# Latent attention: one maximum tile issued after the whole fourth score, and a new assignment of four PSUM areas

## The chip, the core and the metric

The kernel runs on one core of a Trainium2 chip. The metric is the device time of one execution in microseconds (us), the median of several runs. The core has five instruction queues that matter here: the tensor engine (PE, with its weight loads shown apart as PEld), the vector engine (DVE), the scalar engine (ACT), GpSimd (POOL) and the queue that issues DMAs (SP). Each works through its own list in order; semaphores hold an instruction back until what it needs has happened on another engine. PE writes its products to PSUM, which the kernel holds as one tile `PB` of eight banks of 512 fp32 numbers per partition; DVE and ACT read them there.

## The reference, cut to what matters

A stream of 1024 latent tokens and 256 context tokens passes two layers: windowed attention, then multi-head latent attention. The change lies in the second. Its core, for 16 heads and all 1280 keys, is

```
s = (einsum("bqhd,bkhd->bhqk", qn, kn) + einsum("bqhd,bkd->bhqk", qr, kr)).astype(F32) * scale
p = softmax(s, axis=-1)
o = einsum("bhqk,bkhd->bqhd", p, v)
yx = (o * silu(gx)) @ w_out          # then residual and a last rms_norm
```

Only the latent tokens are queries, since no layer follows.

## The kernel before, in words

Layer 2's attention is cut into 32 units (`UnitB`): 16 heads, each with two halves of 512 queries. A unit's work is written as small steps, and the loop over units interleaves steps of neighbouring units by hand. PE, ACT and DVE run in exactly the order in which the code issues instructions (`manual_schedule`), so the text of the loop is the order of the queues. Waits between engines are derived by the framework from the tiles and regions that two instructions share.

The steps of a unit `u`, with `nu` the next one, `nnu` the one after that, and `pu` the one before:

- `top(b)`, for b = 0 to 3: an upper estimate of the scores of 128 queries, one plain product pass. Four matmuls (L1261) fill two banks, `psm`, with the scores against 1024 keys; the matmuls go in pairs, one on the upper and one on the lower 64 rows of the array, side by side. DVE takes the maximum over both banks (`reduce_max`, L1263). For b = 1 and b = 2, four more matmuls of 256 columns (L1269) then fill `rest`, the scores of two query blocks against the other 256 keys, and DVE reduces these too (L1270). For b = 3 a DVE minimum (L1272) joins the two. I call L1261 the maxima's products, and `rest` the paired parts.
- `shift()`: transposes the maxima into `pm_bank` (L1276) and builds the rows that are subtracted inside the score product (L1277, L1282).
- `score(i)`, for i = 0 to 4: 256 keys against 512 queries, five passes of a split-precision product, each a pair of matmuls: ten matmuls (L1298) into a slot of two banks. `score(i, a, b)` issues passes a to b-1 only. After the fifth, ACT takes the exponential of the slot into an SBUF tile (L1304), and POOL adds it to a running sum (L1308, L1312).
- `PV()`: the value product of the unit before, ten fp32 matmuls (L1320, recorded as 20) into `pv_bank`; ACT and DVE read it (L1335, L1339 in `fin` and `fin1`). `fin2` and `fin3` transpose the sums and apply them (L1349, L1364, L1365, L1367).

There are two slots, banks 4 and 5 and banks 6 and 7, handed out in turn by `slot()`: six times per unit (five scores and one scratch slot `x`). So score 0 of a unit takes the slot that score 3 of the unit before used, and score 1 that of score 4. The first matmul into a slot waits until the exponential that last read it is done.

The order on PE in one unit of the loop (L1544 to L1583) is: score 0 passes 0 and 1; `nu.top(2)`; the rest of score 0; score 1; `nu.top(3)`; in two of four units a product that builds the next heads' keys; the value product; the transposes; `nnu.top(0)`; score 2; score 3 passes 0 to 3; `nnu.top(1)`; score 3 pass 4; score 4. Every eighth unit builds values (`make_V`) ahead of `nnu.top(0)`.

The PSUM areas before:

| area | what | banks |
|---|---|---|
| `pv_bank` | value product | 0, all columns |
| `psm` (used part) | maxima's products | 1 and 2 |
| `pm_bank` | transposed maxima | 3, columns 0 to 127 |
| `rest` | paired parts | 0 and 3, columns 256 to 511 |
| `slots` | scores, scratch | 4 and 5, 6 and 7 |

Of the kernel before, what the change touches and what calls it, by code (L numbers as in the profile page):

```python
# [34 lines left out]
class Ring:  # L35
# [6 lines left out]
    def next(self):  # L42
        b = self.bufs[self.i % len(self.bufs)]
        self.i += 1
        return b
# [15 lines left out]
def kernel(ctx: ExitStack, tc: tile.TileContext, t, out, dbg=None):  # L61
# [5 lines left out]
    PB = ppool.tile([128, 8, 512], F32, name="PB")  # L67
# [56 lines left out]
    def mm3(o, a, b, first, last):  # L124
        (ah, al), (bh, bl) = a, b
        nc.tensor.matmul(o, ah, bh, start=first, stop=False)  # L126
        nc.tensor.matmul(o, al, bh, start=False, stop=False)  # L127
        nc.tensor.matmul(o, ah, bl, start=False, stop=last)  # L128
# [1021 lines left out]
    otr = Ring(F, [0, 4], 1024)  # L1150
    rbr = Ring(F, [8, 9], 256)
    mxr = Ring(F, [44, 44.5], 128)
    psm = PB[:, 1:4, :]
    pm_bank = PB[:, 3, 0:128]
    slots = [PB[:, 4:6, :], PB[:, 6:8, :]]
    pv_bank = PB[:, 0, :]
    rest = PB[:, 0:4:3, 256:512]

    def slot():
        slots.reverse()  # L1160
        return slots[1]

    def make_kr():
        for n, c0 in enumerate((0, 4, 8)):
            pt = slot()[:, 0]
            cn = min(4, NT - c0)
            for c in range(cn):
                nc.tensor.transpose(pt[0:32, c * 128 : c * 128 + 128], krF[:, c0 + c, :], ident)
            w = slice(512 * (n // 2), 512 * (n // 2) + 128 * cn)
            ps = [64 * t for t in ((0, 1) if n == 2 else (n,))]  # L1170
            src = pt[0:32, 0 : cn * 128]
            for p in ps:
                nc.scalar.copy(kr1[p : p + 32, w], src)
                nc.scalar.copy(kr2[n // 2][p : p + 32], src)
            for p in ps:
                nc.vector.tensor_sub(kr1[p + 32 : p + 64, w], src, kr1[p : p + 32, w].bitcast(F32))
            yield

    def ones_kr():
        for p in (32, 96):  # L1180
            for kr in kr2:
                n = kr.shape[-1]
                nc.gpsimd.tensor_copy(kr[p : p + 4], const[p : p + 4, 0:1].to_broadcast([4, n]))

    def make_V(quad, x, x0=psm[:, 0:2]):
        for t0, ps in ((0, x0), (4, PB[:, 0:1]), (2, x)):
            nt = min(2, NP - t0)
            for j in range(2 * nt):
                ti = 2 * t0 + j
                o = ps[:, j // 2, (j % 2) * 256 : (j % 2) * 256 + 256]  # L1190
                for k in range(2):
                    mm3(
                        o,
                        [ckvT[:, s, k, ti * 128 : ti * 128 + 128] for s in range(2)],
                        [ukV[:, s, k, quad * 256 : quad * 256 + 256] for s in range(2)],
                        k == 0, k == 1,
                    )
            nc.scalar.copy(
                Vq[:, 2 * t0 : 2 * t0 + 2 * nt].rearrange("p t h d -> p (t h d)"),
                ps[:, 0:nt].rearrange("p a b -> p (a b)"),  # L1200
            )
            yield
# [26 lines left out]
    class UnitB:  # L1229
# [24 lines left out]
        def top(self, b):  # L1254
            n, r1, _ = self.q
            bs = slice(b * 128, b * 128 + 128)
            pairs = ((n[:, 0, bs], self.kt[:, 0]), (r1[:, bs], kr1))
            rs = [slice(64 * t, 64 * t + 64) for t in range(2)]
            for i, (q, k) in enumerate(pairs):
                for t in range(2):  # L1260
                    nc.tensor.matmul(psm[:, t], q[rs[t]], k[rs[t], 0:512], start=i == 0, stop=i == 1)  # L1261
            mx, flat = self.mx, psm[:, 0:2].rearrange("p a b -> p (a b)")
            nc.vector.reduce_max(mx[:, 32 + b : 33 + b], flat, AX.X, negate=True)  # L1263
            if b in (1, 2):
                b0 = b - b % 2
                for i, (q, k) in enumerate(((n[:, 0], self.kt[:, 0]), (r1, kr1))):
                    for t in range(2):
                        c = slice((b0 + t) * 128, (b0 + t) * 128 + 128)
                        nc.tensor.matmul(rest[:, t], q[rs[t], c], k[rs[t], 512:768], start=i == 0, stop=i == 1)  # L1269
                nc.vector.reduce_max(mx[:, 104 + b0 : 106 + b0], rest, AX.X, negate=True)  # L1270
            if b == 3:
                nc.vector.tensor_tensor(mx[:, 32:36], mx[:, 32:36], mx[:, 104:108], ALU.min)  # L1272
# [209 lines left out]

    units = [UnitB(i) for i in range(NU)]
    vk = make_V(0, slots[0], slots[1])
    for m in mxr.bufs:
        nc.vector.memset(m, 0.0)
# [10 lines left out]
    with tc.manual_schedule(engines={E.PE, E.Activation, E.DVE}):  # L1497
        kr = make_kr()
        ones_kr()
        next(kr)  # L1500
        next(kr)
        g_tile(8, 3, 0, pv_bank)
        next(kr)
        g_tile(8, 3, 1)
        make_K(0, (0, 1), slot())
        g_tile(9, 3, 0, psm[:, 0])
        make_K(0, (2,), slot())
        g_tile(9, 3, 1)
        next(vk)
        u0.top(0)  # L1510
        next(vk)
        g_tile(8, 4, 0, slots[0][:, 0])
        u0.top(1)
        next(vk)
        u0.top(2)
        g_tile(8, 4, 1)
        units[2].prep()
        u0.top(3)
        g_tile(9, 4, 0, slots[0][:, 1])
        u0.shift()  # L1520
        u1.top(0)
        make_K(1, (0, 2), slots[1])
        u1.top(1)
        g_tile(9, 4, 1)
        nc.scalar.activation(warm, const[:, 1:2], AF.Exp)
        u1.top(2)
        for ui, u in enumerate(units):
            pu, ppu = [units[ui - n] if ui >= n else None for n in (1, 2)]
            nu, nnu = [units[ui + n] if ui + n < NU else None for n in (1, 2)]
            if nnu and ui:  # L1530
                nnu.prep()
            if ui == 0:
                u.score(0)
                nu.top(3)
                u.score(1)
                nu.shift()
                nnu.top(0)
                u.score(2)
                u.score(3, 0, 4)
                nnu.top(1)  # L1540
                u.score(3, 4, 5)
                u.score(4)
                continue
            u.score(0, 0, 2)  # L1544
            if nu:
                nu.top(2)
            u.score(0, 2, 5)
            u.score(1, hold=True)
            if nu:
                nu.top(3)  # L1550
            x = slot()
            if ui % 4 == 0 and u.pair < 7:
                make_K(u.pair + 1, (0, 2), x)
            if ui % 4 == 1 and u.pair < 7:
                make_K(u.pair + 1, (1,), x)
            if ui == NU - 2:
                next(out_fill)
            pu.PV()
            u.expo(1)
            if ui % 4 > 1 and ui < 23 or ui > 25:  # L1560
                next(wo_fill)
            if ui == NU - 1:
                next(out_fill)
            pu.fin()
            if nu:
                nu.shift()
            if ppu and ppu.e == 1:
                ppu.fin3(x[:, 0])
            pu.fin2(x[:, 1])
            if ui % 8 == 0:  # L1570
                pu.fin1()
                for _ in make_V(u.pair // 2, x):
                    pass
            if nnu:
                nnu.top(0)
            if ui % 8:
                pu.fin1()
            u.score(2)
            u.score(3, 0, 4)
            if nnu:  # L1580
                nnu.top(1)
            u.score(3, 4, 5)
            u.score(4)  # L1583
        u, pu = units[-1], units[-2]
        pu.fin3(slot()[:, 0])
        next(out_fill)
        next(out_fill)
        u.PV()
        u.fin()
        u.fin1()  # L1590
        next(out_fill)
        next(out_fill)
        u.fin2(slot()[:, 0])
        next(out_fill)
        next(out_fill)
        u.fin3(slot()[:, 0])
# [75 lines left out]
```

## Time and profile before

| | |
|---|---|
| median of 3 runs | 1620.67 us (1620.19 to 1623.16) |
| the profiled execution's own time | 1622.09 us |
| its span in the trace | 1620.3 us |
| granted clock of PE, mean | 0.993 |
| PE busy | 1574.6 us, 97% of the span |
| DVE, ACT, POOL busy | 964.9, 803.9, 701.1 us |

The loop over the units lies between about 1025 and 1518 us of the span. In the rows of the trace, L1298 and the like are lines of the kernel; `x4` counts instructions; an arrow `<-` in brackets names what ended an engine's idle time. PE's rows are merged: `x16` from one start to one end are 16 matmuls in a row, eight pairs. A PEld row is the loading of weights that goes ahead of each matmul; a wait for a semaphore shows there. The rows themselves stand in the prediction.

### The profile page before, as it was taken

To read this page: it belongs to the slowest core of one execution; us is meant where nothing else is said; L and a number is where in the kernel's file an instruction comes from. 1 tells how busy PE (TensorE), PEld (TensorE's weight loads), DVE (VectorE), ACT (ScalarE), POOL (GpSimd) and SP (SyncE) were. 2 spreads that over 40 slices of the span, in tenths; PEclk is the share of its full clock that TensorE was granted. 3 is DMA by queue.
4 is the path that set the end of the run, shared out by engine and by line. 5 is a ranking of instruction groups with operands and counts; after the bars stand their busy time and mean duration, and the time that the engine had idled before them with its cause. 6 is when DMAs were issued, how large, how long until landed. Compare 5 with 4: busy or idle time off the path is not lost.

```text
span 1620.3 us, 27188 instructions
## 1 busy us (share of the span) xinstructions
PE 1574.6 (97%) x9938; PEld 1222.6 (75%) x9938; DVE 964.9 (60%) x2089; ACT 803.9 (50%) x1558; POOL 701.1 (43%) x684
## 2 busy tenths in 40 slices
PE   7999999999999999997999999999999999999998
PEld 3787787887878888887998899655666655666587
DVE  3515451538888888878525202677677677677354
ACT  3432232349777777777413333454555554545321
POOL 1231121114543333344104250488687688688510
PEclk8999999999999999999999999999999999999999
DMA  7446765444343333326104753313232323244151
GB/s 249 163 146 200 230 201 174 122 144 112 100 115 92 95 92 92 89 89 217 43 24 120 266 163 92 96 30 101 66 95 82 81 77 95 66 128 116 57 173 65
DMA packets 147206, 192.71 MB, mean 119 GB/s; under 512 B 13936, under 2 KB 84208, under 8 KB 147072
## 3 DMA queue, kind: packets, MB, share of 16 engines
q1 hardware_dynamic: 145456, 188.94, 38.5%
q10 hardware_dynamic: 1616, 2.04, 0.4%
q8 instruction: 78, 1.28, 0.3%
q14 instruction: 56, 0.46, 0.1%
HBM read 144.77 MB, written 46.15 MB: 118 GB/s over the span
## 4 chain that ended last, share of the span: by engine, by line
PE 81%; ACT 6%; DVE 4%; issue 2%; POOL 1%; DMA 1%; ACTq 0%; POOLq 0%; SPq 0%; DVEq 0%
PE PB L126 14%; PE PB L127 14%; PE PB L128 14%; PE PB L1298 10%; PE PB L1320 8%; PE PB L1261 4%; PE PB L621 4%; PE PB L611 3%; PE PB L583 2%; ACT arena_f L1304 2%; PE PB L584 2%; PE PB L181 1%; ACT arena_f L593 1%; PE PB L1269 1%; PE PB L1349 1%
## 5 line engine op out<-in xcount | busy, mean ns | idle before, releaser
L126 PE MATMUL PB<-arena_r 128*128 128x512 f32 (+3 forms) x1496 | 509.8, 342 | 3.7 <-ACT arena_r L387 1.6
L127 PE MATMUL PB<-arena_r 128*128 128x512 f32 (+3 forms) x1496 | 503.5, 337 | 3.4 <-DVE arena_r L388 1.8
L128 PE MATMUL PB<-arena_r 128*128 128x512 f32 (+3 forms) x1496 | 501.3, 335 | 0.2 <-DVE arena_r L122 0.2
L1312 POOL TENSOR_TENSOR arena_f<-arena_f 128x512 f32<-128x512 f32 x252 | 328.6, 1304 | 95.8 <-ACT arena_f L1304 79.6
L126 PEld LDWEIGHTS PB<-arena_r 128*128 128x128 f32 x1496 | 284.4, 191 | 50.9 <-issue 17.2
L127 PEld LDWEIGHTS PB<-arena_r 128*128 128x128 f32 x1496 | 285.4, 191 | 31.6 <-DVE arena_r L388 3.3
L128 PEld LDWEIGHTS PB<-arena_r 128*128 128x128 f32 x1496 | 285.3, 191 | 28.3 <-DVE arena_r L122 0.4
L122 POOL TENSOR_TENSOR arena_r<-arena_f,arena_r 128x512 fp32r<-128x512 f32 x88 | 115.1, 1321 | 308.6 <-ACT arena_r L121 253.2
L1304 ACT ACTIVATE arena_f<-PB 128x1024 f32<-128x1024 f32 x160 | 164.1, 1026 | 123.6 <-PE PB L1298 58.4
L1263 DVE TENSOR_REDUCE arena_f<-PB 128x1 f32<-128x1024 f32 x128 | 156.1, 1219 | 103.1 <-PE PB L1261 102.6
L1298 PE MATMUL PB<-arena_r 64*128 64x512 f32 (+1 forms) x1600 | 211.0, 397 | 2.4 <-ACT arena_f L1304 0.3
L1298 PEld LDWEIGHTS PB<-arena_r 64*128 64x128 f32 (+1 forms) x1600 | 145.6, 186 | 42.9 <-ACT arena_f L1304 16.7
L590 DVE CUSTOM_DVE_ANT_0 arena_f<-PB,arena_f,small 128x256 f32<-128x256 f32 (+1 forms) x288 | 145.2, 523 | 25.4 <-PE PB L584 19.0
L1320 PE MATMUL PB<-arena_f 128*64 128x512 f32 x640 | 144.4, 597 | 0.0
L122 DVE TENSOR_TENSOR arena_r<-PB,arena_r 128x512 fp32r<-128x512 f32 (+1 forms) x186 | 123.2, 671 | 22.1 <-ACT arena_r L121 21.5
L593 ACT ACTIVATE arena_f<-arena_f,small 128x640 f32<-128x640 f32 (+2 forms) x160 | 119.3, 746 | 28.0 <-DVE small L592 26.9
L621 PE MATMUL PB<-arena_r 128*128 128x512 f32 x336 | 123.7, 441 | 3.4 <-ACT arena_f L632 3.1
L121 ACT CAST arena_r<-arena_f 128x512 fp32r<-128x512 f32 (+2 forms) x137 | 82.2, 609 | 80.1 <-DVE arena_f L485 11.5
L121 ACT CAST arena_r<-PB 128x512 fp32r<-128x512 f32 (+1 forms) x186 | 103.9, 569 | 31.7 <-PE PB L611 31.1
L611 PE MATMUL PB<-ident,arena_f 128*128 128x128 f32 x672 | 111.5, 274 | 1.4 <-ACT arena_f L593 0.9
L1320 PEld LDWEIGHTS PB<-arena_f 128*64 128x64 f32 x640 | 43.1, 136 | 83.3 <-issue 82.5
L611 PEld LDWEIGHTS PB<-ident,arena_f 128*128 128x128 f32 x672 | 83.5, 140 | 20.4 <-ACT arena_f L593 5.1
(182 smaller groups left out, 2018.2 us busy)
## 6 DMA issues: line engine op xcount, KB each, us to landing
arena_f<-ada_w SPq DMA_DIRECT2D x47, 512.0 KB, 5.3
arena_r<-q_d SPq DMA_DIRECT2D x80, 256.0 KB, 4.0
arena_r<-qn_d SPq DMA_DIRECT2D x64, 256.0 KB, 3.9
arena_r<-qr_d SPq DMA_DIRECT2D x192, 64.0 KB, 3.3
arena_f<-a_w_in SPq DMA_DIRECT2D x40, 256.0 KB, 3.2
arena_f<-x SPq DMA_DIRECT2D x16, 512.0 KB, 5.5
g_d<-arena_f SPq DMA_DIRECT2D x32, 256.0 KB, 2.1
q_d<-arena_f SPq DMA_DIRECT2D x64, 128.0 KB, 2.4
```

The source lines that it names most:

```text
L121: nc.scalar.copy(hi, src)
L122: (lo_eng or nc.vector).tensor_sub(lo, src, hi.bitcast(F32))
L126: nc.tensor.matmul(o, ah, bh, start=first, stop=False)
L127: nc.tensor.matmul(o, al, bh, start=False, stop=False)
L128: nc.tensor.matmul(o, ah, bl, start=False, stop=last)
L611: nc.tensor.transpose(pt[:, h, :], self.Ps[h][:, ci * 128 : ci * 128 + 128], ident)
L621: nc.tensor.matmul(self.pv, V[:, self.chunks[ci], self.g, :], PT[:, s], start=ci == 0 and s == 0, stop=ci == self.m - 1 and s == 1,)
L1263: nc.vector.reduce_max(mx[:, 32 + b : 33 + b], flat, AX.X, negate=True)
L1298: nc.tensor.matmul(S[:, t], k[r, c : c + 128], q[r], start=j == 0, stop=j == 4)
L1304: nc.scalar.activation(E, self.S, AF.Exp)
L1312: eng.tensor_add(self.acc, self.acc, E[:, t])
L1320: nc.tensor.matmul(self.pv[p : p + 64], Vq[:, cs[t], self.h % 4, :], E[:, t], start=i == 0, stop=i == 4)
```

## The change

`nnu.top(1)` is issued after the whole of score 3 instead of between its fourth and fifth pass, in every unit that has it. The areas in banks 0 to 3 get new places: `psm` banks 2 and 3, `pm_bank` bank 1, and `rest` banks 0 and 1; `pv_bank` stays in bank 0. No instruction is added or removed on any engine.

```diff
-    psm = PB[:, 1:4, :]
-    pm_bank = PB[:, 3, 0:128]
+    psm = PB[:, 2:4, :]
+    pm_bank = PB[:, 1, 0:128]
     slots = [PB[:, 4:6, :], PB[:, 6:8, :]]
     pv_bank = PB[:, 0, :]
-    rest = PB[:, 0:4:3, 256:512]
+    rest = PB[:, 0:2, 256:512]
...
-    def make_V(quad, x, x0=psm[:, 0:2]):
+    def make_V(quad, x, x0=psm):
...
-            mx, flat = self.mx, psm[:, 0:2].rearrange("p a b -> p (a b)")
+            mx, flat = self.mx, psm.rearrange("p a b -> p (a b)")
...
             u.score(2)
-            u.score(3, 0, 4)
+            u.score(3)
             if nnu:
                 nnu.top(1)
-            u.score(3, 4, 5)
             u.score(4)
```

The same edit is made in the branch for the first unit, `ui == 0`.

The order on PE around `nnu.top(1)`, in a unit without a value build. L1261 and L1269 are its matmuls; the rows of L1298 above them are scores 2 and 3, those below the end of score 3 (before) and score 4. `waits` names the engine whose semaphore a matmul waits for.

```order
 L1298 MATMUL PB<-arena_r 128x512 [waits DVE_49]
-L1298 MATMUL PB<-arena_r 128x512 x6
+L1298 MATMUL PB<-arena_r 128x512 x8
 L1261 MATMUL PB<-arena_r 128x512 [waits DVE_49]
 L1261 MATMUL PB<-arena_r 128x512 x3
 L1269 MATMUL PB<-arena_r 128x256 [waits DVE_49]
 L1269 MATMUL PB<-arena_r 128x256 x3
-L1298 MATMUL PB<-arena_r 128x512 x2
 L1298 MATMUL PB<-arena_r 128x512 [waits Activation_49]
 L1298 MATMUL PB<-arena_r 128x512 x9
```

Two matmuls, score 3's fifth pass, went from behind `top(1)` to ahead of it.

The order on PE at `nu.top(2)`, behind the first two passes of the next unit's score 0:

```order
 L1261 MATMUL PB<-arena_r 128x512 [waits DVE_49]
 L1261 MATMUL PB<-arena_r 128x512 x3
-L1269 MATMUL PB<-arena_r 128x256 x4
+L1269 MATMUL PB<-arena_r 128x256 [waits DVE_49]
+L1269 MATMUL PB<-arena_r 128x256 x3
 L1298 MATMUL PB<-arena_r 128x512 x4
```

Nothing moved here, but the paired parts now carry a wait on DVE of their own.

And on PE at `nu.top(3)` and the value product behind it:

```order
 L1261 MATMUL PB<-arena_r 128x512 [waits DVE_49]
 L1261 MATMUL PB<-arena_r 128x512 x3
-L1320 MATMUL PB<-arena_f 64x512 x10
+L1320 MATMUL PB<-arena_f 64x512 [waits DVE_49]
+L1320 MATMUL PB<-arena_f 64x512 x9
```

Here too the order is the same, and the value product has a wait on DVE of its own.

More of the change, by code (lines that the diff above doesn't have):

```diff
@@ L1578 @@
             u.score(2)
-            u.score(3, 0, 4)
+            u.score(3)
             if nnu:
                 nnu.top(1)
-            u.score(3, 4, 5)
             u.score(4)
```

## The prediction

> **What bounds the kernel now.** I read the page's chain of waits and the table by stretches first.
>
> ```profile
> PE 81%; ACT 6%; DVE 4%; issue 2%; POOL 1%; DMA 1%; ACTq 0%; POOLq 0%; SPq 0%; DVEq 0%
> 1033.00:1495.00 462.00, 459.91 (x3263) 289.85 (x3261) 325.65 (x385) 235.87 (x307) 359.65 (x279) 1.00 0.30 82
> ```
>
> In the loop over units (second row; the busy columns are PE, PEld, DVE, ACT, POOL, then the clock) PE looks busy for 459.9 of 462 us, DVE for 325.7 and POOL for 359.7. PE's matmul ends are modelled and stretch over short stalls, so what PE loses is seen at its weight loads. Their waits from 1000 to 1560 us (total, times, longest):
>
> ```profile
> PEld PB L1298 <- ACT arena_f L1304: 16.7, 34, 0.7
> PEld PB L1261 <- DVE arena_f L1270: 9.7, 31, 1.9
> PEld PB L1269 <- DVE arena_f L1339: 5.4, 19, 0.4
> PEld PB L1261 <- DVE arena_f L1263: 0.8, 4, 0.2
> ```
>
> About once per unit a score waits for an exponential, and once a maximum tile waits for the reduction of the paired parts. So small stalls of an otherwise full PE are all there is to gain or lose. The timeline of one unit shows the first kind:
>
> ```profile
> 1250.41 1.22 DVE L1263 TENSOR_REDUCE arena_f<-PB 128x1 f32<-128x1024 f32 x1
> 1251.43 1.03 ACT L1304 ACTIVATE arena_f<-PB 128x1024 f32<-128x1024 f32 x1 [1.01 <-PE PB L1298]
> 1252.08 0.62 PE L1261 MATMUL PB<-arena_r 64*128 64x512 f32 x4
> 1252.53 0.40 PE L1269 MATMUL PB<-arena_r 64*128 64x256 f32 x4
> 1252.73 1.23 DVE L1263 TENSOR_REDUCE arena_f<-PB 128x1 f32<-128x1024 f32 x1 [0.39 <-PE PB L1261]
> 1252.76 2.40 PE L1298 MATMUL PB<-arena_r 36*128 36x512 f32 x16
> 1253.34 2.15 ACT L1304 ACTIVATE arena_f<-PB 128x1024 f32<-128x1024 f32 x2 [0.88 <-PE PB L1298]
> 1253.87 0.68 DVE L1270 TENSOR_REDUCE arena_f<-PB 128x2 f32<-128x512 f32 x1
> 1254.41 0.30 PEld L1298 LDWEIGHTS PB<-arena_r 64*128 64x128 f32 x4 [0.53 <-ACT arena_f L1304]
> ```
>
> `top(1)` (1252.08, 1252.53) stands between the fourth and fifth pass of score 3. So the exponential of score 3 starts only at 1253.34 and ends some 1.03 later; the next unit's score 0, which takes the same slot, gets its weights at 1254.41 after 0.53 of waiting.
>
> **The change part by part.** Nothing is added or removed, so the whole sum is stalls. The unit of time is a pair of matmuls. The same unit, PE alone, with the next one's shapes, and one row of the chain:
>
> ```profile
> 1254.99 0.63 PE L1261 MATMUL PB<-arena_r 64*128 64x512 f32 x4
> 1255.46 0.40 PE L1269 MATMUL PB<-arena_r 64*128 64x256 f32 x4
> 1255.70 2.01 PE L1298 MATMUL PB<-arena_r 64*128 64x512 f32 x16
> 1257.56 0.72 PE L1261 MATMUL PB<-arena_r 64*128 64x512 f32 x4
> 1258.21 4.51 PE L1320 MATMUL PB<-arena_f 128*64 128x512 f32 x20
> 1265.99 0.63 PE L1261 MATMUL PB<-arena_r 64*128 64x512 f32 x4
> 1266.52 0.50 PE L1269 MATMUL PB<-arena_r 64*128 64x256 f32 x4
> 1266.86 2.33 PE L1298 MATMUL PB<-arena_r 36*128 36x512 f32 x16
> ...
> 1255.87 1.85 PE PB L1298 x16
> ```
>
> Sixteen matmuls without a stall take 1.85 on the chain, so a pair takes 0.23; four of L1269 take 0.23 (1255.46 to 1255.70).
>
> *(a) Score 3's exponential.* A run of 16 matmuls takes 2.01 unstalled, but 2.40 (1252.76) and 2.33 (1266.86) across the unit boundary: 0.39 and 0.32 lost, the wait and a slower second pair behind it. Now the new order, in the unit at 1252. The fifth pass moves to 1252.08, and `top(1)` to 1252.31. The exponential began 0.58 after the fifth pass (1252.76 to 1253.34), so it now begins at 1252.66; ACT's exponential of score 2 is over by then (1251.43 + 1.03 = 1252.46). It ends at 1253.69, and adding 0.05 for the release, the slot is free at 1253.74. PE meanwhile: `top(1)` 0.46 and 0.23, so score 4 starts at 1253.00, its five pairs end at 1254.16, and the next score 0 asks for weights one pair ahead, at 1253.93. That is 0.19 after the slot is free: the stall goes. Boundaries with a `top(1)`: 30 (of the 34 waits, the others I put in the last two units, which have none). 30 x 0.35, the mean of the two shapes: 10.5 us.
>
> *(b) Top 3 behind the paired parts.* DVE's part of this place, in the unit before:
>
> ```profile
> 1241.76 1.23 DVE L1263 TENSOR_REDUCE arena_f<-PB 128x1 f32<-128x1024 f32 x1 [1.11 <-PE PB L1261]
> 1242.90 0.68 DVE L1270 TENSOR_REDUCE arena_f<-PB 128x2 f32<-128x512 f32 x1
> 1243.63 0.30 PEld L1261 LDWEIGHTS PB<-arena_r 64*128 64x128 f32 x4 [0.26 <-DVE arena_f L1270]
> ```
>
> `top(3)` writes `psm` (banks 1 and 2), which L1263 had read by 1242.99; yet its weights come only when L1270, which reads banks 0 and 3, is done (1243.58). The framework takes the stretch from bank 0 to bank 3 as one region. With `rest` in banks 0 and 1 and `psm` in 2 and 3 the wait falls back to L1263: the waits of their own that L1269 and L1320 now carry would be superfluous if L1261 still covered L1270. Four such matmuls take 0.72 after the wait (1257.56) and 0.63 without (1254.99): 30 x 0.10 = 3.0 us. The value product now waits for L1270 itself; it begins 0.65 after `top(3)` (1257.56 to 1258.21), when L1270 is over.
>
> *(c) Paired parts behind the value product's reader.* In the unit at 1265.99, L1269 starts 0.53 after L1261, elsewhere 0.47 (1254.99 to 1255.46), and takes 0.50, elsewhere 0.40: 0.16 lost to L1339, which reads bank 0. With `top(1)` 0.23 later this wait has passed. I count 7 such units, every fourth; the other short ones of the 19 waits cost no time. A harder shape stands in 4 units:
>
> ```profile
> 1221.94 0.70 PE L1261 MATMUL PB<-arena_r 64*128 64x512 f32 x4
> 1222.63 0.50 PE L1269 MATMUL PB<-arena_r 64*128 64x256 f32 x4
> ```
>
> 0.69 instead of 0.47, and 0.50 instead of 0.40: 0.32. 7 x 0.16 + 4 x 0.32 = 2.4 us.
>
> *(d) The start of the loop.*
>
> ```profile
> 1022.73 1.23 DVE L1263 TENSOR_REDUCE arena_f<-PB 128x1 f32<-128x1024 f32 x1
> 1023.87 0.68 DVE L1270 TENSOR_REDUCE arena_f<-PB 128x2 f32<-128x512 f32 x1
> 1024.60 0.30 PEld L1261 LDWEIGHTS PB<-arena_r 64*128 64x128 f32 x4 [1.95 <-DVE arena_f L1270]
> 1020.00:1024.50 4.50, 2.86 (x24) 2.65 (x23) 4.27 (x8) 2.45 (x5) 0.00 (x0) 1.00 0.09 31
> 1024.50:1028.60 4.10, 4.00 (x24) 3.26 (x26) 1.87 (x3) 0.97 (x3) 0.00 (x0) 0.58 0.71 207
> ```
>
> Here the same wait lasts 1.95. L1261 may now start after L1263, at 1024.01 instead of 1024.60, and L1269 behind it at about 1024.66 instead of 1024.94 (1024.60 plus two slow pairs): 0.3 us. Behind the wait the clock is at 0.58 for 4.1 us, which costs 4.1 x 0.42 = 1.7. A wait of 1.35 may not trip it; I leave that out of the sum and keep it for the range. The Trainium skill's page "TensorE: Matmul & The Clock Gate", section "What's actually happening", says that the clock halves after at least one idle window of about 3.4 us; by it a wait of 1.95 should not have tripped it, so here the trace shows more than the rule, and the rule gives no gain for shortening the wait.
>
> *(e) What the change adds.* `top(1)` is one pair nearer to `top(2)`, and what is queued behind `top(2)` on PE is all the rest. In the new order L1263 of `top(1)` starts 0.65 after its products (1252.08 to 1252.73), at 1252.96, and ends at 1254.19; L1270 starts 1.14 later than L1263 and ends at 1254.78. `top(2)` would start its matmuls at 1254.16 + 0.46 = 1254.62, and asks for weights at 1254.39: needed by 1254.24, 0.15 to spare. Its paired parts ask at 1254.85 and L1270 releases them at 1254.83: 0.02 to spare. Bounds: nothing, or, if it is missed by a little each time, the slow second pair of (b), 0.10 x 30 = 3.0 us. I take 0.5, because a load that is late by less than its 0.23 of lead delays no matmul:
>
> ```profile
> 1251.66 0.68 DVE L1339 TENSOR_TENSOR arena_f<-PB,arena_f 64x512 f32<-64x512 f32 x1
> ```
>
> this released L1269's weights only at 1252.40, and L1269 still ran in step at 1252.53.
>
> Next in line: score 1 waits for score 4's exponential. The row at 1253.34 holds two exponentials and ends at 1255.49, no later in the new order; score 1 asks at about 1255.77 (`top(2)` at 1254.62, its 0.69, three pairs of score 0, one pair ahead). `top(3)` asks at 1256.93, and its L1263, 0.37 earlier than now, ends near 1256.5. Nothing else is near.
>
> Sum: 10.5 + 3.0 + 2.4 + 0.3 - 0.5 = 15.7 us. The profiled execution took 1622.09, 1.4 above the median: 1606.4 on its scale, 1605.0 on the median's.
>
> **The rivals.** *The thin margin fails* (e): `top(2)`'s paired parts, or the maxima before them, wait in every unit, 0.10 to 0.25: 3 to 7 us given back, 1608 to 1612. For it speaks the 0.02; against it that L1263's length hardly varies:
>
> ```profile
> L1263 DVE TENSOR_REDUCE arena_f<-PB x128: 1171/1225/1226, 999.7 to 1497.5; 128x1 f32<-128x1024 f32 x128
> ```
>
> *The banks free nothing*: `top(2)`, now one pair nearer, still waits for L1270. Its weights come at 1254.83 instead of 1254.39: a loss of 0.44 less the 0.23 of lead, and 0.10 for the pair behind, 0.31 x 30 = 9.3, and (b) stays. 10.5 + 2.4 - 9.3 leaves 3.6, so about 1617. Against it: the new waits in the built order.
>
> *Slower: POOL becomes the bound.* Its rows in this unit and by line:
>
> ```profile
> 1246.72 1.28 POOL L1308 TENSOR_TENSOR arena_f<-arena_f 128x512 f32<-128x512 f32 x1
> 1252.60 4.02 POOL L1312 TENSOR_TENSOR arena_f<-arena_f 128x512 f32<-128x512 f32 x3 [1.56 <-ACT arena_f L1304]
> L1312 POOL TENSOR_TENSOR arena_f<-arena_f 128x512 f32<-128x512 f32 x252 | 328.6, 1304 | 95.8 <-ACT arena_f L1304 79.6
> ```
>
> Nine additions a unit at 1.30 are 11.7, and the transposes (L1349) wait for the last. A unit is 13.9 now (1240.52 to 1254.41, the two score stalls' ends) and 13.4 after. POOL decides once an addition takes over 13.4 / 9 = 1.49; to be slower than before it must pass 1.54. At 1.6 the unit is 14.4, and 30 x 0.5 gives 1635. Against it: POOL idles 1.56 ahead of 1252.60.
>
> ```profile
> 1240.52 0.30 PEld L1298 LDWEIGHTS PB<-arena_r 64*128 64x128 f32 x4 [0.54 <-ACT arena_f L1304]
> ```
>
> **How the numbers follow.** Forecast 0.74 (0.2 of it with the clock's 1.7 on top, near 1603); thin margin 0.16; banks free nothing 0.05; POOL 0.05. The forecast's own spread is the means in (a) and (c), 2 us, and the clock: 1602 to 1608. The range takes in the thin margin: 1601.5 to 1611. A measurement here can tell about 0.2%, 3.2 us, from no change. Faster: forecast, thin margin, and half of the third: 0.92; same 0.04; slower 0.04.
>
> **What would show it.** In the changed profile the waits of PEld L1298 for L1304 should fall from 16.7 us to about 2, those of L1261 for L1270 to nearly nothing, and runs of 16 matmuls across the boundary should take 2.0. If L1269 shows waits of 0.1 or more for L1270, the margin failed; if L1261 still waits for L1270, the banks did nothing; if L1349 waits for L1312, POOL is the bound. I am wrong at the root if these waits go and the time does not follow.

## The result, and the profile after

| | before | changed |
|---|---|---|
| median of 5 runs | 1620.19 us (1619.92 to 1623.16) | 1604.28 us (1602.29 to 1607.61) |
| ratio | | 0.9902, 95% interval 0.9886 to 0.9917 |
| the profiled execution's span | 1620.3 us | 1605.8 us |

The change made the kernel faster by 0.98%, 15.9 us (13.4 to 18.5 by the interval). The prediction was 1605.0 in a range of 1601.5 to 1611. The waits of the changed kernel's weight loads from 1000 to 1560 us (total, times, longest), the rows that answer to the four shown of before:

```profile
PEld PB L1298 <- ACT arena_f L1304: 1.8, 4, 0.7
PEld PB L1261 <- DVE arena_f L1263: 1.6, 2, 1.3
PEld PB L1269 <- DVE arena_f L1339: 0.9, 4, 0.2
PEld PB L1269 <- DVE arena_f L1270: 0.3, 1, 0.3
```

The exponential's wait fell from 16.7 us in 34 to 1.8 in 4, that for L1339 from 5.4 to 0.9. The 4 waits for the exponential that are left lie in the last two units, where the prediction put them. L1261 no longer waits for L1270 anywhere; what is left at that place is the start of the loop, with waits of 1.35 and 0.23 for L1263. PE of one unit, in the timeline of the changed kernel:

```profile
1243.16 2.47 PE L1298 MATMUL PB<-arena_r 64*128 64x512 f32 x20
1245.47 0.63 PE L1261 MATMUL PB<-arena_r 64*128 64x512 f32 x4
1245.94 0.40 PE L1269 MATMUL PB<-arena_r 64*128 64x256 f32 x4
1246.18 1.80 PE L1298 MATMUL PB<-arena_r 64*128 64x512 f32 x14
1247.82 0.63 PE L1261 MATMUL PB<-arena_r 64*128 64x512 f32 x4
1248.29 0.40 PE L1269 MATMUL PB<-arena_r 64*128 64x256 f32 x4
1248.53 2.02 PE L1298 MATMUL PB<-arena_r 64*128 64x512 f32 x16
1250.39 0.63 PE L1261 MATMUL PB<-arena_r 64*128 64x512 f32 x4
1250.94 4.51 PE L1320 MATMUL PB<-arena_f 128*64 128x512 f32 x20
```

Scores 2 and 3 now run as 20 matmuls, and the run across the unit's end is 14 long: 1.80, which is the unstalled 2.02 of 16 less one pair. `top(3)` takes 0.63 where it took 0.72.

Where the time came from is read from the loop: the first and last start of the score products, in the view of line L1298, of before and of the changed kernel.

```profile
L1298 PE MATMUL PB<-arena_r x1600: 383/392/626, 1025.7 to 1518.4; 64*128 64x512 f32 x142, 36*128 36x512 f32 x36
```

```profile
L1298 PE MATMUL PB<-arena_r x1600: 383/392/501, 1026.6 to 1503.7; 64*128 64x512 f32 x142, 36*128 36x512 f32 x36
```

492.7 us became 477.1: 15.6 less. The spans differ by 14.5. Ahead of the loop the changed kernel's execution falls 1.7 us behind the one of before (0.4 near 480 us of the span, the rest mostly between 720 and 745), in work that the change does not touch; why is not known. At the start of the loop 0.8 comes back, and 0.2 is lost behind the loop. Since such differences arise outside the loop, its length is the finer measure below.

### The profile page after: what moved, and what is told of

It reads as the page before. It is cut to its first block, busy times and chain, and to the rows that moved or that the text cites. A ratio compares the mean times of both kernels' runs of the same rounds, so it can differ in the third digit from the quotient of the medians.

```text
span 1605.8 us, 27188 instructions
## 1 busy us (share of the span) xinstructions
PE 1562.9 (97%) x9938; PEld 1226.4 (76%) x9938; DVE 943.9 (59%) x2089; ACT 804.6 (50%) x1558; POOL 702.2 (44%) x684
## 4 chain that ended last, share of the span: by engine, by line
PE 82%; DVE 5%; ACT 4%; issue 2%; POOL 1%; DMA 1%; POOLq 0%; SPq 0%; DVEq 0%; ACTq 0%
PE PB L126 14%; PE PB L127 14%; PE PB L128 14%; PE PB L1298 11%; PE PB L1320 8%; PE PB L1261 4%; PE PB L621 4%; PE PB L611 3%; PE PB L583 2%; PE PB L584 2%; ACT arena_f L593 1%; PE PB L181 1%; PE PB L1269 1%; DVE arena_r L122 1%; ACT arena_r L121 1%
## 5 line engine op out<-in xcount | busy, mean ns | idle before, releaser
L127 PE MATMUL PB<-arena_r 128*128 128x512 f32 (+3 forms) x1496 | 502.9, 336 | 2.8 <-DVE arena_r L388 1.2
L1263 DVE TENSOR_REDUCE arena_f<-PB 128x1 f32<-128x1024 f32 x128 | 156.1, 1219 | 86.6 <-PE PB L1261 86.5
L1298 PE MATMUL PB<-arena_r 64*128 64x512 f32 (+1 forms) x1600 | 202.2, 392 | 0.4 <-ACT arena_f L1304 0.3
L1298 PEld LDWEIGHTS PB<-arena_r 64*128 64x128 f32 (+1 forms) x1600 | 145.9, 185 | 31.6 <-ACT arena_f L1304 1.8
L590 DVE CUSTOM_DVE_ANT_0 arena_f<-PB,arena_f,small 128x256 f32<-128x256 f32 (+1 forms) x288 | 145.2, 522 | 25.2 <-PE PB L584 18.7
```

Source lines behind the costliest of these rows:

```text
L1298: nc.tensor.matmul(S[:, t], k[r, c : c + 128], q[r], start=j == 0, stop=j == 4)
```

## The experiments

Each kernel below differs from the changed kernel, or from before, by the diff shown. "Loop" is the distance from the first to the last start of L1298 in its profiled execution.

The runs were taken on three occasions, each with its own runs of before, so compare the ratios rather than the medians.

| kernel | median, us | ratio to before, 95% | loop, us |
|---|---|---|---|
| before | 1620.23 to 1621.07 | 1 | 492.7 |
| changed, again | 1606.21 | 0.9905 (0.9891 to 0.9918) | 477.0 |
| banks only | 1617.22 | 0.9975 (0.9965 to 0.9985) | 488.4 |
| order only | 1619.41 | 0.9982 (0.9974 to 0.9991) | 489.3 |
| `top(1)` one pair later | 1617.89 | 0.9981 (0.9972 to 0.9990) | 488.7 |
| `top(1)` two pairs later | 1624.50 | 1.0025 (1.0015 to 1.0035) | 495.9 |
| `top(2)` one pair later | 1606.07 | 0.9911 (0.9898 to 0.9925) | 477.2 |
| `top(2)` one pair earlier | 1610.17 | 0.9928 (0.9914 to 0.9943) | 479.2 |
| first unit reordered | 1605.50 | 0.9905 (0.9891 to 0.9918) | see there |
| one more POOL addition | 1611.96 | 0.9945 (0.9930 to 0.9960) | 482.3 |
| two more POOL additions | 1636.24 | 1.0094 (1.0080 to 1.0108) | 505.9 |

### The two parts apart

The changed kernel was measured again beside its two parts.

> The changed kernel itself, beside the parts of it on the same chip. My theory: 1604 us, 0.990 of the kernel before. The small stalls add up to about 6 us in the loop over units, and its first score of a unit no longer waits for an exponential. No theory expects another number; it is the base for the other three.

It came out at 0.9905, its loop at 477.0.

Banks only: the old order with the new areas.

```diff
-    psm = PB[:, 1:4, :]
-    pm_bank = PB[:, 3, 0:128]
+    psm = PB[:, 2:4, :]
+    pm_bank = PB[:, 1, 0:128]
...
-    rest = PB[:, 0:4:3, 256:512]
+    rest = PB[:, 0:2, 256:512]
```

> The new banks with the old order of score 3 and the second maximum tile. My theory: only the wait of top 3 and the wait at the start of the loop go, 30 x 0.10 + 0.3 = 3.3 us, so about 1617 (0.998); the waits of L1298 for L1304 stay near 16.7 us, those of L1269 for L1339 near 5.4. If the parts were independent with the order as the whole gain, 1620. If the banks carried the gain by themselves, 1605.

Order only: the new order with the old areas.

```diff
             u.score(2)
-            u.score(3, 0, 4)
+            u.score(3)
             if nnu:
                 nnu.top(1)
-            u.score(3, 4, 5)
             u.score(4)
```

> The new order with the old banks. My theory: the exponential's wait goes (10.5 us) and the one of the paired parts behind L1339 (2.4), but top 2, now one pair nearer, waits for L1270: 0.31 x 30 = 9.3 us back, and top 3 goes on waiting. So 3.6 us gained, about 1616.6 (0.998), and L1261 waiting for L1270 twice per unit, about 60 times, 15 to 20 us in all at the weight loads. If the parts were independent, 13 us gained: 1607. If the false wait costs nothing: 1605.

Banks only gained 0.25%, 4.0 us, where 3.3 was expected; order only 0.18%, 2.9 us, where 3.6 was expected. The waits of the banks-only kernel:

```profile
PEld PB L1298 <- ACT arena_f L1304: 16.7, 34, 0.7
PEld PB L1269 <- DVE arena_f L1339: 5.3, 18, 0.4
PEld PB L1261 <- DVE arena_f L1263: 2.4, 6, 1.4
```

and of the order-only kernel:

```profile
PEld PB L1261 <- DVE arena_f L1270: 24.9, 62, 1.9
PEld PB L1298 <- ACT arena_f L1304: 1.8, 4, 0.7
PEld PB L1269 <- DVE arena_f L1339: 0.9, 4, 0.3
```

The banks take away the wait for L1270 and leave the other two; at the start of the loop a wait of 1.4 for L1263 stands in its place. The order takes away the exponential's wait and that for L1339, but the wait for L1270 now comes twice per unit (62 times, 24.9 us; 15 to 20 were expected). One of the second kind, at `top(2)` of the order-only kernel:

```profile
1252.40 1.22 DVE L1263 TENSOR_REDUCE arena_f<-PB 128x1 f32<-128x1024 f32 x1 [0.64 <-PE PB L1261]
1253.54 0.68 DVE L1270 TENSOR_REDUCE arena_f<-PB 128x2 f32<-128x512 f32 x1
1254.28 0.30 PEld L1261 LDWEIGHTS PB<-arena_r 64*128 64x128 f32 x4 [0.49 <-DVE arena_f L1270]
```

L1263 had read the maxima's banks by 1253.62; the weights came at 1254.28, behind L1270. So the parts are worth 4.0 and 2.9 us alone and 15.9 together: with the old banks the order's gain turns into a new wait, and it is the banks that remove it. That L1270's wait came from the two areas' places is shown; the prediction's word for why, that the framework takes banks 0 to 3 as one region, is an inference from the waits in the built order and these rows.

### How thin the margin ahead of top 2 is

`top(1)` one pair later, and two pairs later (`u.score(4, 0, 2)` and `u.score(4, 2, 5)`):

```diff
             u.score(3)
+            u.score(4, 0, 1)
             if nnu:
                 nnu.top(1)
-            u.score(4)
+            u.score(4, 1, 5)
```

> The changed kernel with top 1 one pair of matmuls later still, behind the first pass of score 4. It takes 0.23 off the margins of 0.15 (maxima) and 0.02 (paired parts) ahead of top 2. My theory: the paired parts' weights come 0.21 late, inside the lead of 0.23, but the second pair behind them is late by 0.09: 30 x 0.09 = 2.7 us slower than the changed kernel, about 1607, and L1269 waiting for L1270 in every unit, some 0.2 each. If the thin margin is already used up, each unit loses the whole 0.23 more: 7 us, about 1611. If the margin is larger than I worked out: 1604, no waits.

> The changed kernel with top 1 two pairs later, behind the second pass of score 4. 0.46 off the margins: the maxima's weights at top 2 come 0.31 late (0.08 beyond the lead, and 0.10 for the pair behind), the paired parts' 0.26 late (0.03 beyond the lead, and 0.10). My theory: 0.3 x 30 = 9 us slower than the changed kernel, about 1613. If the margin is much larger than I worked out: no slower than with one pair. If it is used up already: 0.46 x 30 = 14 us, 1618.

Both expectations missed: 0.9981 and 1.0025, with loops 11.6 and 18.8 us longer than the changed kernel's, where 2.7 and 9 were expected. The first one's waits, and its PE with the weight load of score 4:

```profile
PEld PB L1298 <- ACT arena_f L1304: 16.5, 34, 0.7
PEld PB L1269 <- DVE arena_f L1270: 8.2, 31, 0.3
```

```profile
1244.80 3.01 PE L1298 MATMUL PB<-arena_r 64*128 64x512 f32 x22
1247.32 0.19 PEld L1298 LDWEIGHTS PB<-arena_r 64*128 64x128 f32 x2 [0.47 <-ACT arena_f L1304]
1250.22 0.49 PE L1269 MATMUL PB<-arena_r 64*128 64x256 f32 x4
```

The last of these rows is what was expected, 0.49 instead of 0.40: 30 x 0.09 = 2.7. What the first two show was overlooked. Twenty matmuls take 2.47 and 22 should take 2.70, but took 3.01: score 4 starts where `top(1)` stood, and its slot is the one that score 2's exponential is still reading. 30 x 0.31 = 9.3, and 9.3 + 2.7 = 12.0 against 11.6. Two pairs later the same wait is there (16.4 us in 34). With 9.3 taken off, that kernel loses 9.5, where 9 was worked out for the margin alone; besides L1269 its maxima now wait, as expected:

```profile
PEld PB L1261 <- DVE arena_f L1263: 12.3, 32, 1.3
```

So of the four places tried, `top(1)` has one good one: behind score 3, whose exponential is then not held up, and ahead of score 4, where it fills the time of score 2's.

That the two causes were split rightly was tested with `top(2)` moved earlier, which takes the same 0.23 off the margin and leaves score 4 in place:

```diff
-            u.score(0, 0, 2)
+            u.score(0, 0, 1)
             if nu:
                 nu.top(2)
-            u.score(0, 2, 5)
+            u.score(0, 1, 5)
```

> The changed kernel with top 2 one pair of matmuls earlier, behind one pass of score 0 instead of two. Like moving top 1 later by a pair, it takes 0.23 off the margins of 0.15 and 0.02, but score 4 keeps its place, so the wait for score 2's exponential that came with that move must be absent. My theory: 30 x 0.10 = 3 us slower than the changed kernel, about 1608 (0.992), with L1269 waiting for L1270 in every unit and no wait of L1298 for L1304 beyond the changed kernel's 1.8 us. If the loss of the run with top 1 a pair later lay mostly in the thin margin and not in the exponential: 12 us slower, 1617.

The loop is 2.1 us longer than the changed kernel's, the ratio 0.9928 against 0.9902 and 0.9905, some 4 us. Its waits:

```profile
PEld PB L1269 <- DVE arena_f L1270: 7.6, 31, 0.3
PEld PB L1298 <- ACT arena_f L1304: 1.8, 4, 0.7
```

One pair less of margin costs 2 to 4 us by itself, without a wait for the exponential. And does the changed kernel already pay for it? `top(2)` one pair later, the opposite edit:

```diff
-            u.score(0, 0, 2)
+            u.score(0, 0, 3)
             if nu:
                 nu.top(2)
-            u.score(0, 2, 5)
+            u.score(0, 3, 5)
```

> The changed kernel with top 2 one pair later, behind three passes of score 0 instead of two: both margins ahead of it grow by 0.23, the one ahead of top 3 falls from 0.35 to 0.12. My theory: no stall is left to take there and none comes: 1604, the changed kernel's time. If the thin margin costs something in the changed kernel, up to 3 us faster: 1601. If the margin ahead of top 3 is smaller than worked out, 3 us slower with L1261 waiting for L1263.

0.9911, the loop 477.2: no difference. The margin of 0.02 costs nothing in the changed kernel.

### POOL as the rival bound

```diff
-                nc.gpsimd.tensor_add(self.acc, E[:, 0], E[:, 1])
+                for _ in range(2):
+                    nc.gpsimd.tensor_add(self.acc, E[:, 0], E[:, 1])
```

(`range(3)` in the second kernel.)

> The changed kernel with one more addition of 1.3 us on POOL per unit: the first addition of a unit is made twice, with the same result. My theory: POOL needs about 12.4 us of a unit of 13.4, and the units that build keys last 15.5 to 16; over four units 57 of 59 us, so 0 to 2 us slower, 1604 to 1606. If POOL is the bound already: 32 x 1.3 = 42 us, 1646.

> The changed kernel with two more such additions on POOL per unit: the first addition is made three times. My theory: over four units POOL needs 62 us where PE takes 59, so POOL is the bound in most of the loop: 7 to 25 us slower, 1611 to 1629, with L1349 waiting for L1312. If POOL is far from being the bound: 1604. If it is the bound already: 84 us, 1688.

One more addition costs 0.9945 against 0.9902 to 0.9905, some 7 us, and 5.2 in the loop; 0 to 2 was expected, 42 by the rival. Counted from the first score product, the first 29 of the 32 value products start within 0.1 us of the changed kernel's: up to there the addition is hidden. The loss comes in two places in the last units (line numbers above 1308 are one higher in this kernel; L1350 is `fin2`'s transpose). At the first, the last unit's `top(0)` waits for its queries:

```profile
1476.56 0.18 PEld L1261 LDWEIGHTS PB<-arena_r 64*128 64x128 f32 x1 [0.73 <-DMA arena_r<-qn_d]
```

With shorter waits beside it this costs 1.6. The DMAs that bring the queries are issued on SP about 2.9 us behind a store, in the kernel with one more addition and in the changed kernel:

```profile
1466.68 0.34 SPq L1369 DMA_DIRECT2D og_d<-arena_f  x1
1463.35 0.34 SPq L1368 DMA_DIRECT2D og_d<-arena_f  x1
```

The store goes 0.02 to 0.03 after POOL's multiplication of what it stores, so by these rows POOL's backlog reaches PE through the DMA queue. The second place is a wait for POOL itself, here and in the changed kernel:

```profile
1504.62 0.42 PEld L1350 LDWEIGHTS PB<-ident,arena_f 128*128 128x128 f32 x4 [3.79 <-POOL arena_f L1313]
1499.17 0.42 PEld L1349 LDWEIGHTS PB<-ident,arena_f 128*128 128x128 f32 x4 [1.12 <-POOL arena_f L1312]
```

and in the table by stretches of the kernel with one more addition, just behind it:

```profile
1505.90:1509.30 3.40, 3.40 (x20) 2.65 (x18) 1.01 (x3) 1.74 (x3) 3.24 (x3) 0.50 0.34 130
```

Here, where no next unit's work covers POOL's backlog, PE waits 2.67 longer than in the changed kernel and then runs 3.4 us at half the clock (0.50, the value behind the five engines), which costs 1.7; a wait of 0.7 for an exponential falls away. That is 3.7, and with the 1.6 it makes 5.3 against the loop's 5.2.

Two more additions cost 1.9%, 31 us (28.8 in the loop; 7 to 25 was expected). The transposes wait for POOL 18.7 us in 13 waits, 17.6 more than in the changed kernel. The expectation had left out the clock: at or just behind such waits it is at 0.50 for 3.4 us from 1119.5, 1249.2 and 1378.9, and for 6.8 us from 1491.6 and 1522.3. That is 23.9 us at half the clock, a loss of 11.9, and 17.6 + 11.9 = 29.5 against 28.8. So POOL was not the bound at a unit of 13.5: one addition more costs PE time only at the loop's end, two cost it all along the loop. The prediction's point of decision, 1.49 us per addition instead of 1.30, is 1.7 us more per unit over nine additions, and lies between the 1.3 of one and the 2.6 of two.

### What is left at the loop's start

The longest waits left are 1.3 us for L1263 ahead of the second unit's `top(2)` and 1.4 for L1272 ahead of its shift. Reordering the first unit was meant to fill them:

```diff
         nc.scalar.activation(warm, const[:, 1:2], AF.Exp)
-        u1.top(2)
...
                 u.score(0)
+                nu.top(2)
+                u.score(1)
                 nu.top(3)
-                u.score(1)
+                u.score(2)
                 nu.shift()
                 nnu.top(0)
-                u.score(2)
                 u.score(3)
```

> The changed kernel with the first unit reordered: its score 0 ahead of the second unit's top 2, and its score 2 ahead of that unit's shift, so that 1.35 us of waiting for L1263 and about 1 us of waiting for L1272 are filled; behind it the third unit's top 1 stands only one score from its top 0 and should wait about 0.4. My theory: 1.5 to 2 us faster than the changed kernel, 1602 to 1604, with the first maxima's product to the last score's 2 us nearer. If the vector engine's backlog there sets the pace: no change.

0.9905, the changed kernel's ratio. From the first maxima's product to the last score's it takes 502.9 us (999.2 to 1502.1) against 503.1 (1000.6 to 1503.7): 0.2 instead of 1.5 to 2. Its start:

```profile
1023.88 0.99 PEld L1298 LDWEIGHTS PB<-arena_r 64*128 64x128 f32 x9 [0.62 <-ACT arena_f L1091]
1027.08 0.30 PEld L1261 LDWEIGHTS PB<-arena_r 64*128 64x128 f32 x4 [0.36 <-DVE arena_f L1263]
1029.72 0.13 PEld L1276 LDWEIGHTS PB<-ident,arena_f 128*100 128x100 f32 x1 [1.16 <-DVE arena_f L1272]
```

The first score now waits for ACT, which has not yet read the projection (L1091) in its slot; `top(3)`, one score behind `top(2)`, waits for DVE; the shift waits for L1272 as before; and the third unit's `top(1)` waits 0.63 for L1263, where 0.4 was expected. The waits moved. No run beat the changed kernel.

## Why the prediction was right

- **What bounds the kernel**: small stalls on PE, once or twice per unit. Both parts' kernels show each wait going with its own edit, and the changed kernel shows them gone together.
- **(a) and (c), 12.9 us**: 1.6 too high. From the banks-only kernel to the changed one, which differ by the order alone, the loop falls from 488.4 to 477.1: 11.3. The starts of the matmuls tell the two apart. In banks only the 30 score runs across the boundary take 10.2 us more than 0.231 per pair; that is 0.34 each, so the mean of the two shapes, 0.35, was right. In the changed kernel 0.5 of it is left: (a) gave about 9.6 of the 10.5. The matmuls of the 30 `top(1)` take 23.2 and then 21.5 us: (c) gave about 1.7 of the 2.4, as four units go on waiting for L1339 (0.9 us).
- **(b), 3.0 us**: from before to banks only the loop falls by 4.3. Of these the half clock at the loop's start, in before's execution alone, takes about 1.4, the part of its 1.7 that lies behind the first score product; about 2.9 is left. The prediction's own rows, 0.72 and 0.63, give 0.09 per unit and not 0.10, so 2.7.
- **(d), 0.3 us**: it lies ahead of the first score product, so it is not in the loop's 15.6. In the changed kernel

```profile
1025.69 0.30 PEld L1261 LDWEIGHTS PB<-arena_r 64*128 64x128 f32 x4 [1.35 <-DVE arena_f L1263]
1026.29 0.30 PEld L1269 LDWEIGHTS PB<-arena_r 64*128 64x128 f32 x4 [0.30 <-DVE arena_f L1270]
```

  the wait at the loop's start fell from 1.95 to 1.35, and 0.30 for L1270 came behind it, as worked out. The half clock that followed in before did not follow in the changed kernel. But it did not follow in the order-only kernel either, which waits 1.95 there as before does. So the shorter wait is not shown to be the reason, and it was right to keep the 1.7 out of the sum.
- **(e)**: 0.5 us was taken off for the thin margin, and nothing was lost (`top(2)` a pair later gains nothing). The working of the margin stands: in the changed kernel

```profile
1246.15 1.23 DVE L1263 TENSOR_REDUCE arena_f<-PB 128x1 f32<-128x1024 f32 x1 [0.64 <-PE PB L1261]
1247.29 0.68 DVE L1270 TENSOR_REDUCE arena_f<-PB 128x2 f32<-128x512 f32 x1
1247.58 0.43 PEld L1261 LDWEIGHTS PB<-arena_r 64*128 64x128 f32 x4
1248.06 0.42 PEld L1269 LDWEIGHTS PB<-arena_r 64*128 64x128 f32 x4
```

  L1263 ends at 1247.38, and adding 0.05, top 2's weights at 1247.58 have 0.15 to spare; L1270 ends at 1247.97, and L1269's at 1248.06 have 0.04. Predicted were 0.15 and 0.02.
- **The rivals**: the thin margin is real but held. "The banks free nothing" is refuted by the banks-only kernel; what it priced, 3.6 us for the order with the wait left in place, is the order-only kernel, which gained 2.9. POOL is not the bound, and the point that the prediction gave for it fits the kernels with one and two additions more.

The mechanism was right, but that the sum of 15.7 and the measured 15.9 agree so well is partly luck: the order's terms were 1.6 too high, the margin's deduction 0.5 too high, and the 1.4 of the half clock, which was left out, is in the loop's 15.6 of the profiled executions but not surely in the medians' 15.9.

## What to carry to other kernels

A reordering that frees one engine can put two of another's steps too near to each other; price both in the same unit, here pairs of matmuls, before choosing the place, and list every user of a shared slot, since the place that was best lay between one score's exponential and another's. Where a wait seems to have no cause in the data, see whether a strided view spans what lies between its pieces, as was inferred here: moving the pieces together was worth 4.0 us alone, and let the order have its 12 more. Two parts that gain 0.25% and 0.18% alone gained 0.98% together, so testing them one by one would have undervalued both.

## What the runs showed of the hardware

The four-column minimum on DVE (L1272) took a quarter of its time after the change, though nothing of it was changed. By line, from 1030 to 1530 us, of before:

```profile
L1272 DVE TENSOR_TENSOR arena_f<-arena_f 128x4 f32<-128x4 f32 x31 | 33.7, 1089 | 1.1
```

and of the changed kernel (measured again: 255 ns; banks only: 1029; order only: 987):

```profile
L1272 DVE TENSOR_TENSOR arena_f<-arena_f 128x4 f32<-128x4 f32 x31 | 8.2, 263 | 1.1
```

It reads two operands from SBUF, and it ends when the POOL addition beside it does. In before:

```profile
1245.67 1.12 DVE L1272 TENSOR_TENSOR arena_f<-arena_f 128x4 f32<-128x4 f32 x1
1238.69 8.07 POOL L1312 TENSOR_TENSOR arena_f<-arena_f 128x512 f32<-128x512 f32 x6 [1.17 <-ACT arena_f L1304]
```

and in the changed kernel:

```profile
1238.83 0.23 DVE L1272 TENSOR_TENSOR arena_f<-arena_f 128x4 f32<-128x4 f32 x1
1235.03 5.35 POOL L1312 TENSOR_TENSOR arena_f<-arena_f 128x512 f32<-128x512 f32 x4
```

The sixth addition of before ends at 1246.76 and the minimum at 1246.79; after the change the third of four ends at 1239.04 (three times 1.34 behind 1235.03), the minimum at 1239.06. So it is in all 31 rows of either kernel: the minimum ends 0.02 to 0.03 behind the addition that it started beside. In banks only, five minima start just behind an addition's end, and take 0.16. The two parts together, and neither alone, moved the minimum to just ahead of the end. The Trainium skill's page "SBUF — State Buffer", section "SBUF: two separate sides", says that DVE and GpSimd share a pair of SBUF ports as an exclusive lock, held for a whole instruction, which a DVE instruction with two SBUF inputs needs too, against a GpSimd instruction that reads SBUF. These rows agree. In most units it costs no time, as the value product covers the minimum. The first unit has no value product: there the shift waits 1.4 for L1272 in the changed kernel, of which the minimum itself took 0.72.
